# Activation buffers of 1280 instead of 1152 bytes, and operands of two stages placed in older buffers

## The chip, the cores and the metric

The kernel runs on one core of one Trainium2 chip. The metric is the device time of one execution in microseconds. The three runs before the change took 1665.74 to 1665.91 us, median 1665.88.

## The reference

One inference step (one layer) of a decoder with three parallel branches. Two groups of tokens share the weights: 256 of a prompt and 8 x 4 of samples, so all products have 288 columns.

```python
h = rms_norm(x, g_mix);  proj = h @ w_in
u_lin, u_gate, q_sb, k_sb, v_sb, q_mem, gate_logits = split(proj)
c = silu(layer_norm(causal_conv31(u_lin * sigmoid(u_gate))));  y_conv = c @ w_conv_out
y_sb  = stick_breaking_attention(q_sb, k_sb, v_sb, past pages) @ w_sb_out    # 8 heads
y_mem = softmax_attention(q_mem, memory) @ w_mem_out                         # 4 heads
g = sigmoid(gate_logits + b_gate)                                            # 3 x 2048
x = x + (g[0]*y_conv + g[1]*y_sb + g[2]*y_mem) @ w_o
x = x + square(relu(rms_norm(x, g_mlp) @ w_up)) @ w_down                     # 2048 -> 8192 -> 2048
```

All in float32. Besides the two groups' outputs the new keys and values, the last convolution inputs and the memory keys and values are returned.

## The kernel before

**Products.** Features lie on the 128 partitions, tokens along the free dimension (T = 288). Each float32 operand is split into a high part, rounded to fp32r, and the remainder, and a product is made of three: high x high, high weight x low activation, low weight x high activation. The weights stream from memory as 504 slabs of 128 x 1024 (8 blocks of 128 x 128), once each. `load_slab` brings one into a `wr` buffer; ScalarE rounds it (`cast_weights`, L295) into `wh`; VectorE subtracts (`sub_part`, L306) into `wl`. Four buffers of each rotate, so TensorE can be up to four slabs behind.

`main_tile` makes one 128 x 288 output tile in a PSUM bank (`pm`, four of them) from two slabs. `products` goes through a slab in 24 matmuls: for each of the 8 blocks the high weights with `a.h` and `a.l`, then the 8 low blocks with `a.h`. `chunk` (L467) issues them; the activation is the moving operand, 128 x 288, and the weight block the stationary one. Then an `evac` of VectorE, ScalarE or GpSimd empties the bank.

**Stages**, in the order of `main`: the memory's keys and values (`mem_products`, L518, in which the weights are the moving operand); the convolution's inputs; the heads of the memory attention and of the stick-breaking attention; the three gated branches (`branch_products` 2, 1, 0, in groups of four gates and four branch tiles); w_o (`out_tile`); and four times a block of 16 up tiles and 16 down tiles. The attentions over samples, the depthwise convolution (124 VectorE operations, L691 and L693) and the normalizations run beside them.

**Order.** A planner (`Order`) writes the order of the program: each piece of work is a generator that asks for an engine, a duration, flags that must be set, and buffers of a pool (`a=2`); the one that can start first is emitted. `give` returns buffers. Engines work in the order in which instructions were emitted.

**Buffers.** A pool holds equal buffers per partition. In address order: the constants, `wr` (4 of 4096 bytes), `a` (81 of 1152 bytes, one 288-column float32 tile each), `t` (11 of 1152, working tiles), `k4` (9 of 4096, pages of the caches), `s` (8 of 2048, attention rows), `wh` and `wl` (4 of 4096 each). `Acts` is a pair of `a` buffers for the high and low part. `hx` (the normalized input) holds 32 of them up to the last branch, `omem` and `osb` (the attentions' outputs) 8 and 16, `cact` (the convolution's) 8, `macc` (the gated sum, `branch`, L1229) 16; `merged` (L1242) takes 32. In the feed-forward `x1` holds 16, `h2` 32, and `u`, the squared output of `up_tile` (L1296 to L1304), 32, so that 80 of 81 are taken. `k4` and `s` serve the attentions and the convolution and are idle afterwards.

Of the kernel before, what the change touches and what calls it, by code (L numbers as in the profile page):

```python
# [7 lines left out]
F32 = mybir.dt.float32  # L8
F32R = mybir.dt.float32r
# [5 lines left out]
P = 128  # L15
D_MODEL = 2048
KT = D_MODEL // P
# [4 lines left out]
T = NP + NS  # L22
# [52 lines left out]
class Order:  # L75
# [15 lines left out]
    def add(self, gen, rank, at=None):  # L91
        job = Job(gen, rank, self.now.ready if at is None and self.now else at or 0.0)
        self.jobs.append(job)
        was, self.now = self.now, job
        self.step(job)
        self.now = was
# [10 lines left out]
    def give(self, pool, n=1):  # L107
        self.pools[pool] += [self.now.ready] * n
# [45 lines left out]
def dve(n, *flags, **take):  # L154
    return Ask("DVE", 0.18 + n / 920.0, flags, **take)


def act(n, *flags, **take):
    return Ask("ACT", 0.22 + n / 1200.0, flags, **take)


def pool(n, *flags, **take):
    return Ask("POOL", 0.3 + n / 420.0, flags, **take)


def pe(us, *flags, **take):
    return Ask("PE", us, flags, **take)


def sp(*flags, **take):  # L170
    return Ask("SP", 0.45, flags, **take)


VISIT = 4
MM = 0.1325
MM_MEM = 0.226
# [3 lines left out]
def tile_decoder_step(ctx: ExitStack, tc: tile.TileContext, xT, memT, wall, cvec, kmat, ptab,  # L180
# [1 line left out]
                      yT, oK, oV, oCp, oCs, oMK, oMV):  # L182
    nc = tc.nc
    PS = bass.MemoryType.PSUM
    bufs = {"wr": 4, "w": 4, "a": 81, "t": 11, "k4": 9, "s": 8, "pm": 4, "pa": 3, "pl": 1}

    def open_pool(name, n, space=None):
        if space is None:
            return ctx.enter_context(tc.tile_pool(name=name, bufs=n))
        return ctx.enter_context(tc.tile_pool(name=name, bufs=n, space=space))  # L190

    cpool = open_pool("const", 1)
    pools = {p: open_pool(p, n, PS if p in ("pm", "pa", "pl") else None) for p, n in bufs.items() if p != "w"}
    pools["wh"] = open_pool("wh", bufs["w"])
    pools["wl"] = open_pool("wl", bufs["w"])
    order = Order(bufs)
    give, add, done = order.give, order.add, order.set
# [3 lines left out]
    def tl(p, shape, dt=F32):  # L201
        cnt[0] += 1
        return pools[p].tile(shape, dt, tag=p, name=f"{p}_{cnt[0]}")
# [60 lines left out]
    class Slab:  # L264
        def __init__(self, parts):
            self.parts = parts
            self.landed = [Flag() for _ in range(parts)]
            self.split = [Flag() for _ in range(parts)]
# [12 lines left out]
    def due(s):  # L281
        return at_slab[1] + 2.9 * (s - at_slab[0])
# [32 lines left out]
    class Acts:  # L315


        def __init__(self, n=T):
            self.h, self.l = tl("a", [P, T], F32R)[:, :n], tl("a", [P, T], F32R)[:, :n]
            self.flag = Flag()  # L320

    hm, hx = [None] * KT, [None] * KT
# [305 lines left out]
    lin_done, gat_done, conv_done = ([Flag() for _ in range(CT)] for _ in range(3))  # L628
# [314 lines left out]
    def load_tiles(load, tiles, flags, which):  # L943
        for b in which:
            yield Ask("SP", 1.05, (pages_in,), k4=1)
            t, kb = load(b)
            tiles.append(t)
            flags[b].at = order.landed(kb) + 1.0
# [10 lines left out]
    def read_pages():  # L959

        for i in range(2 * NB):
            yield Ask("SP", 0.6, (pt_in,), 2.5)
            pages.append(nc.sync.value_load(pt[0:1, i:i + 1], min_val=0, max_val=kpool.shape[0] - 1))
        done(pages_in)
# [9 lines left out]
    def sample_values(load, aex, psum, x_T, new, first, cost):  # L974

        tiles, flags = [], [Flag() for _ in range(NB)]
        add(load_tiles(load, tiles, flags, range(0, VISIT)), 2)
        yield from x_T
        add(load_tiles(load, tiles, flags, range(VISIT, NB)), 2)
        if new is not None:  # L980
            yield from new
        for b in range(NB):
            if b % VISIT == 0:
                yield pe(VISIT * cost, *flags[b:b + VISIT], **({} if b else {"pl": 1}))
            if b == 0:
# [10 lines left out]
    def samples():  # L996
# [4 lines left out]
        for b in range(NB):  # L1001
            if b % VISIT == 0:
                yield pe(VISIT * 0.55, *flags[b:b + VISIT], *qm_made, **({} if b else {"pl": 1}))
            if b == 0:
# [30 lines left out]
    osb_in = [Flag() for _ in range(SH)]  # L1035
# [170 lines left out]
        yield from out_rows(out[0], [osb[h] for h in hs], [osb_in[h] for h in hs])  # L1206


    gates = {(br, j): Sigmoid() for br in range(3) for j in range(KT)}

    def gate(br, j):
# [9 lines left out]
    merged = [None] * KT  # L1221

    def branch(br, j):
        def evac(ps):
            sig = gates[br, j]
            if br == 2:
                yield dve(T, sig.flag, a=1)
                macc[j] = tl("a", [P, T])
                nc.vector.tensor_mul(macc[j], ps, sig.out)  # L1229
                give("pm")  # L1230
                give("t")
                return
            yield dve(T, sig.flag)
            nc.vector.tensor_mul(sig.out, ps, sig.out)  # L1234
            give("pm")
            yield dve(T)
            nc.vector.tensor_add(macc[j], macc[j], sig.out)
            give("t")
            if br == 0:
                yield act(T, a=2)  # L1240
                a = merged[j] = Acts()
                nc.scalar.copy(a.h, macc[j])  # L1242
                yield dve(T)
                nc.vector.tensor_sub(a.l, macc[j], a.h.bitcast(F32))
                give("a")
                done(merged_in[j])
        return evac
# [44 lines left out]
    def up_tile(u, f):  # L1292
        def evac(ps):
            yield dve(T, r2_done, t=1)
            r = tl("t", [P, T])
            nc.vector.scalar_tensor_tensor(r, ps, 0.0, r2, op0=ALU.max, op1=ALU.mult)  # L1296
            give("pm")
            yield pool(T)
            nc.gpsimd.tensor_mul(r, r, r)  # L1299
            yield act(T, a=2)  # L1300
            a = Acts()
            nc.scalar.copy(a.h, r)  # L1302
            yield dve(T)
            nc.vector.tensor_sub(a.l, r, a.h.bitcast(F32))  # L1304
            give("t")
            u[f].h, u[f].l = a.h, a.l
            done(u[f].flag)
        return evac
# [48 lines left out]
    def warm_up():  # L1357

        yield pe(4.2, pa=1)
        junk = bank("pa")  # L1360
        for i in range(7):
            nc.tensor.matmul(junk, warm[:, :P], warm[:, :512], start=True, stop=True)  # L1362
        give("pa")
        give("w")

    def main():
        yield from warm_up()
        yield from mem_products()
        yield from conv_products([evac_lin(0, "pa"), evac_gat(0, "pa"), evac_lin(1, "pm"), evac_gat(1, "pm")])
        for j in range(2, CT):  # L1370
            yield from main_tile(hx, evac_lin(j, "pm"))
            yield from main_tile(hx, evac_gat(j, "pm"))
        add(samples(), 3.0)
        for h in range(MH):
            yield from main_tile(hx, mem_head(h), 2 + 0.05 * h)
        for h in range(SH):
            yield from main_tile(hx, sb_key(h), 2.2 + 0.05 * h)
            yield from main_tile(hx, sb_query(h), 2.2 + 0.05 * h)
            yield from main_tile(hx, sb_head(h), 2.2 + 0.05 * h)
        yield from branch_products(2, [Late(omem, h, om_in[h]) for h in range(MH)])  # L1380
        give("a", 8)
        yield from branch_products(1, [Late(osb, h, osb_in[h]) for h in range(SH)])
        give("a", 16)
        yield from branch_products(0, [Late(cact, j, cact_flags[j]) for j in range(CT)])
        give("a", 40)
        mg = [Late(merged, j, merged_in[j]) for j in range(KT)]
        for j in range(KT):
            load, evac = out_tile(j)
            add(load(), 2)
            yield from main_tile(mg, evac)  # L1390
        give("a", 32)
        add(sum_norm(sq_sum, D_MODEL, r2, r2_done, sums_2), 0.4)
        hh = [Late(h2, j, h2_in[j]) for j in range(KT)]
        for c in range(D_FF // D_MODEL):
            u = [Later() for _ in range(KT)]
            for f in range(KT):
                yield from main_tile(hh, up_tile(u, f))
            for j in range(KT):
                yield from main_tile(u, down_tile(j, c == D_FF // D_MODEL - 1))
            give("a", 32)  # L1400

    def setup():
        yield dve(P, km_in)
# [4 lines left out]
    with tc.manual_schedule():  # L1408
        add(loads(), 1.0)
        add(cast_weights(), lambda: 0 if due(cast_at[0]) - order.free["ACT"] < 6.0 else 4.5)  # L1410
        add(mem_norm(), 0.6)
        add(sum_norm(x_sum, D_MODEL, rx, rx_done, sums_x), 0.6)
        add(main(), 20.0)
        add(conv_norm(), 8.0)
        add(setup(), 1.0)
        add(read_pages(), 4.0)
        order.run()
    assert slab_no[0] == wall.shape[0], slab_no

# [155 lines left out]
```

## Time and profile before

| | |
|---|---|
| median of three runs | 1665.88 us |
| profiled execution | 1665.56 us, its span 1663.8 us |
| TensorE busy | 1659.3 us (100%), 12,786 matmuls, granted clock 1.00 |
| VectorE, ScalarE, GpSimd busy | 992.3, 740.5, 138.9 us (60%, 45%, 8%) |
| memory traffic | 297.05 MB read, 6.32 MB written, 182 GB/s |
| weight rounding L295 | 520 on ScalarE, 1022 ns each |
| weight subtraction L306 | 520 on VectorE, 1195 ns each |

In the profile a line such as `L467 PE MATMUL pm<-a,wh 128*128 128x288 f32 x7744` names the line of the kernel, the engine, the operation, the output and the inputs by pool, the shape, and the number of instructions; behind it stand the busy time, the mean duration, and the idle time of the engine before these instructions with what ended it. PE is TensorE's matmul, PEld its weight load, DVE VectorE, ACT ScalarE, POOL GpSimd. The duration of a matmul is modelled and overlaps with the next one's. In the view by stages each row is a stretch of time: its length, TensorE's busy time with the number of its instructions in flight, its granted clock, the share and the rate of the DMA engines. In the timeline a row is a group of like instructions: start, length, name, count.

### The profile page before, as it was taken

The page shows a single profiled execution, that of the slowest core. Times are in us where ns is not written, and L with a number is a line of the kernel's source. Part 1 is how long each engine was busy: PE and PEld are TensorE (multiplying, and loading weights), DVE is VectorE, ACT ScalarE, POOL GpSimd, SP SyncE. Part 2 cuts the span into 40 slices and gives each one's busy share as a digit, 9 for nine tenths or more (in the row PEclk, how much of TensorE's full clock was granted, in tenths as well). Part 3 has the DMA queues.
Part 4 walks back from the last instruction along what each step waited for, and adds up shares of the span by engine and source line. Part 5 has one row for each costly group of instructions (what it writes and reads, how often), then busy time and mean ns, then how long its engine had stood idle before and what let it go on. Part 6 is the DMA issues. An engine that isn't in the chain of part 4 may idle for free.

```text
span 1663.8 us, 30938 instructions
## 1 busy us (share of the span) xinstructions
PE 1659.3 (100%) x12786; PEld 1639.9 (99%) x12786; DVE 992.3 (60%) x1470; ACT 740.5 (45%) x1071; POOL 138.9 (8%) x105
## 2 busy tenths in 40 slices
PE   9999999999999999999999999999999999999999
PEld 7999999999999999999999999999999999999999
DVE  8889888876777655565455544455444554445443
ACT  8746766644434534444443333333333333333332
POOL 0020000000000000001222200121001210022100
PEclk9999999999999999999999999999999999999999
DMA  9676464677755555556555555555555555555562
GB/s 335 210 178 248 140 215 155 200 244 278 285 186 166 167 171 166 165 156 203 186 172 165 166 168 163 166 167 171 161 168 164 166 166 166 165 165 165 177 189 98
DMA packets 107103, 305.39 MB, mean 184 GB/s; under 512 B 19922, under 2 KB 29522, under 8 KB 106962
## 3 DMA queue, kind: packets, MB, share of 16 engines
q1 hardware_dynamic: 106818, 303.39, 57.6%
q8 instruction: 100, 1.64, 0.4%
q14 instruction: 41, 0.34, 0.1%
q10 hardware_dynamic: 144, 0.02, 0.0%
HBM read 297.05 MB, written 6.32 MB: 182 GB/s over the span
## 4 chain that ended last, share of the span: by engine, by line
PE 100%; POOL 0%; DVE 0%; issue 0%; POOLq 0%
PE pm L467 93%; PE pm L518 3%; PE pa L467 1%; PE pl L991 1%; PE pl L1162 0%; PE pa L828 0%; PE pa L829 0%; PE pa L827 0%; PE pl L1007 0%; PE pa L1362 0%; PE pa L801 0%; PE pa L882 0%; PE pa L1118 0%; PE pa L1115 0%; PE pa L1117 0%; PE pa L1081 0%
## 5 line engine op out<-in xcount | busy, mean ns | idle before, releaser
L467 PE MATMUL pm<-a,wh 128*128 128x288 f32 x7744 | 1119.6, 295 | 0.0
L467 PEld LDWEIGHTS pm<-a,wh 128*128 128x128 f32 x7744 | 1057.5, 188 | 2.6 <-issue 2.4
L295 ACT CAST wh<-wr 128x1024 fp32r<-128x1024 f32 (+1 forms) x520 | 529.9, 1022 | 665.6 <-PE pm L467 623.2
L306 DVE TENSOR_TENSOR wl<-wr,wh 128x1024 fp32r<-128x1024 f32 (+1 forms) x520 | 619.8, 1195 | 203.6 <-ACT wh L295 202.3
L467 PE MATMUL pm<-a,wl 128*128 128x288 f32 x3872 | 598.4, 295 | 0.0
L467 PEld LDWEIGHTS pm<-a,wl 128*128 128x128 f32 x3872 | 541.7, 188 | 0.2 <-issue 0.2
L1299 POOL TENSOR_TENSOR t<-t 128x288 f32<-128x288 f32 x64 | 96.2, 1503 | 613.6 <-DVE t L1296 613.6
L1313 DVE TENSOR_TENSOR a<-a,pm 128x288 f32<-128x288 f32 x64 | 29.1, 454 | 127.3 <-PE pm L467 127.3
L1296 DVE SCALAR_TENSOR_TENSOR t<-pm,r 128x288 f32<-128x288 f32 x64 | 29.3, 457 | 97.4 <-PE pm L467 97.4
L1302 ACT CAST a<-t 128x288 fp32r<-128x288 f32 x64 | 27.6, 432 | 133.6 <-POOL t L1299 133.6
L1215 DVE TENSOR_TENSOR t<-pm,rx 128x288 f32<-128x288 f32 x48 | 22.0, 458 | 76.0 <-PE pm L467 75.9
L1304 DVE TENSOR_TENSOR a<-t,a 128x288 fp32r<-128x288 f32 x64 | 29.2, 458 | 63.4 <-ACT a L1302 63.4
L693 DVE SCALAR_TENSOR_TENSOR a<-a,cv,a 128x256 f32<-128x256 f32 x120 | 59.6, 496 | 1.5
L1285 POOL TENSOR_TENSOR t<-t,t 128x288 f32<-128x288 f32 x15 | 21.7, 1449 | 395.4 <-ACT t L1282 395.4
L518 PE MATMUL pm<-wh,a 128*128 128x512 f32 x128 | 35.9, 403 | 0.0
L518 PEld LDWEIGHTS pm<-wh,a 128*128 128x128 f32 x128 | 24.4, 193 | 6.3 <-ACT wh L295 0.9
L931 POOL MEMSET k<- 128x1024 f32 x6 | 5.7, 951 | 275.4 <-PE pl L1162 214.0
L1234 DVE TENSOR_TENSOR t<-pm,t 128x288 f32<-128x288 f32 x32 | 14.6, 458 | 21.1 <-PE pm L467 15.0
L1270 DVE TENSOR_TENSOR a<-pm,t 128x288 f32<-128x288 f32 x16 | 7.3, 458 | 29.9 <-PE pm L467 29.9
L219 ACT ACTIVATE t<-t,cv 128x288 f32<-128x288 f32 x48 | 21.8, 524 | 0.0
L518 PE MATMUL pm<-wl,a 128*128 128x512 f32 x64 | 20.3, 398 | 0.0
L680 POOL TENSOR_TENSOR k<-a,cv 128x992 f32<-128x992 f32 x4 | 10.9, 2741 | 74.0 <-DVE a L666 74.0
(198 smaller groups left out, 643.3 us busy)
## 6 DMA issues: line engine op xcount, KB each, us to landing
wr<-in_wall SPq DMA_DIRECT2D x488, 512.0 KB, 3.6
wr<-in_wall SPq DMA_DIRECT2D x32, 256.0 KB, 4.8
k<-in_kpool SPq DMA_DIRECT2D x32, 256.0 KB, 6.0
k<-in_vpool SPq DMA_DIRECT2D x32, 256.0 KB, 5.8
k<-in_mkc SPq DMA_DIRECT2D x8, 512.0 KB, 10.1
k<-in_mvc SPq DMA_DIRECT2D x8, 512.0 KB, 6.5
t<-in_xT SPq DMA_DIRECT2D x16, 144.0 KB, 3.7
out_yT<-a SPq DMA_DIRECT2D x16, 144.0 KB, 1.8
```

The lines of the kernel that those rows point to most:

```text
L219: nc.scalar.activation(out, src, func, **kw)
L295: nc.scalar.copy(sl.h[:, c], sl.raw[:, c])
L306: nc.vector.tensor_sub(sl.l[:, c], sl.raw[:, c], sl.h[:, c].bitcast(F32))
L467: nc.tensor.matmul(ps, w, a, start=(first and i == 0), stop=(last and i == len(todo) - 1))
L518: nc.tensor.matmul(ps[m], x[:, m * P:(m + 1) * P], y[:, w], start=(k == 0 and j < 2), stop=(k == KT - 1 and j in (4, 5)))
L693: nc.vector.scalar_tensor_tensor(c[:, :NP], up[:, k:k + NP], w, c[:, :NP], op0=ALU.mult, op1=ALU.add)
L1215: nc.vector.tensor_mul(g, ps, rx)
L1296: nc.vector.scalar_tensor_tensor(r, ps, 0.0, r2, op0=ALU.max, op1=ALU.mult)
L1299: nc.gpsimd.tensor_mul(r, r, r)
L1302: nc.scalar.copy(a.h, r)
L1304: nc.vector.tensor_sub(a.l, r, a.h.bitcast(F32))
L1313: nc.vector.tensor_add(x1[j], x1[j], ps)
```

## The change

An activation buffer of pool `a` gets 320 columns (1280 bytes) of which 288 are used, and there are 75 of them, not 81. A buffer of 128 bytes that nothing uses is put ahead of `t`. The operands `merged` and `u`, 32 tiles in turn, no longer come from `a`: once the convolution and the attentions over samples are done, `make_homes` takes all nine `k4` buffers, three operands in each at steps of 1280 bytes, and all eight `s` buffers, one in each, and makes sixteen fixed pairs (`homes`) of the first 32 parts. `branch` (for the last of the three branches) writes `merged[j]` to `homes[j]`; `up_tile` writes `u[f]` to `homes[f]`. The instructions that compute are the same ones.

```diff
+APART = 320
-    bufs = {"wr": 4, "w": 4, "a": 81, "t": 11, "k4": 9, "s": 8, "pm": 4, "pa": 3, "pl": 1}
+    bufs = {"wr": 4, "w": 4, "a": 75, "t": 11, "k4": 9, "s": 8, "pm": 4, "pa": 3, "pl": 1}
...
-    pools = {p: open_pool(p, n, PS if p in ("pm", "pa", "pl") else None) for p, n in bufs.items() if p != "w"}
+    pools = {}
+    for p, n in bufs.items():
+        if p == "t":
+            open_pool("gap", 1).tile([P, 32], F32, name="gap")
+        if p != "w":
+            pools[p] = open_pool(p, n, PS if p in ("pm", "pa", "pl") else None)
...
-            self.h, self.l = tl("a", [P, T], F32R)[:, :n], tl("a", [P, T], F32R)[:, :n]
+            self.h, self.l = tl("a", [P, APART], F32R)[:, :n], tl("a", [P, APART], F32R)[:, :n]
...
+    def make_homes():
+        yield sp(*conv_done, *osb_in, k4=bufs["k4"], s=bufs["s"])
+        parts = []
+        for _ in range(bufs["k4"]):
+            x = tl("k4", [P, 1024], F32R)
+            parts += [x[:, i * APART:i * APART + T] for i in range(3)]
+        for _ in range(bufs["s"]):
+            parts.append(tl("s", [P, 512], F32R)[:, :T])
+        for j in range(KT):
+            homes.append(Home(parts[2 * j], parts[2 * j + 1]))
+        done(homes_in)
...
-                yield act(T, a=2)
-                a = merged[j] = Acts()
+                yield act(T, homes_in)
+                a = merged[j] = homes[j]
...
-            yield act(T, a=2)
-            a = Acts()
+            yield act(T)
+            a = homes[f]
...
-        give("a", 32)
...
-            give("a", 32)
...
+        add(make_homes(), 1.0)
```

More of the change, by code (lines that the diff above doesn't have):

```diff
@@ L1206, in sb_sample, with __init__ @@
         yield from out_rows(out[0], [osb[h] for h in hs], [osb_in[h] for h in hs])
+    homes, homes_in = [], Flag()
+    class Home:
+        def __init__(self, h, l):
+            self.h, self.l = h, l
+    def make_homes():
[9 more added lines that the diff above has]
+        done(homes_in)
     gates = {(br, j): Sigmoid() for br in range(3) for j in range(KT)}
```

## The prediction

> **What bounds the kernel now.** I read the page first: the busy times, the granted clock, the chain that ended last, the costliest groups.
>
> ```profile
> span 1663.8 us, 30938 instructions
> PE 1659.3 (100%) x12786; PEld 1639.9 (99%) x12786; DVE 992.3 (60%) x1470; ACT 740.5 (45%) x1071; POOL 138.9 (8%) x105
> ...
> PEclk9999999999999999999999999999999999999999
> ...
> PE pm L467 93%; PE pm L518 3%; PE pa L467 1%; PE pl L991 1%; PE pl L1162 0%; PE pa L828 0%; PE pa L829 0%; PE pa L827 0%; PE pl L1007 0%; PE pa L1362 0%; PE pa L801 0%; PE pa L882 0%; PE pa L1118 0%; PE pa L1115 0%; PE pa L1117 0%; PE pa L1
> ...
> L467 PE MATMUL pm<-a,wh 128*128 128x288 f32 x7744 | 1119.6, 295 | 0.0
> L467 PEld LDWEIGHTS pm<-a,wh 128*128 128x128 f32 x7744 | 1057.5, 188 | 2.6 <-issue 2.4
> ```
>
> TensorE is never out of work: 100% busy, clock not throttled, no idle time before a matmul, and 94% of the chain is one line, L467, the 128x288 product. VectorE (60%) and ScalarE (45%) have room. So the time is the number of matmuls times their pace. The 295 ns of a row is a modelled, overlapped duration; the pace is the distance from one start to the next, which I took from the starts of all matmuls in the trace. The groups of L467 give the count:
>
> ```profile
> L467 PE MATMUL pm<-a,wh x7744: 288/295/406, 52.3 to 1659.2; 128*128 128x288 f32 x199
> L467 PE MATMUL pm<-a,wl x3872: 288/294/402, 52.8 to 1660.3; 128*128 128x288 f32 x194
> L467 PE MATMUL pa<-a,wh x64: 288/294/378, 50.7 to 74.9; 128*128 128x288 f32 x64
> L467 PE MATMUL pa<-a,wl x32: 288/295/298, 51.2 to 75.2; 128*128 128x288 f32 x32
> ```
>
> Together 11,712. For 11,591 of them the next matmul is L467 too and starts within 160 ns; these intervals sum to 1536.1 us, mean 132.52 ns. The other 121 stand at transposes, samples, and a few waits, nearly all in the first 480 us.
>
> Is the pace the same everywhere? The busy time by stage, with the stages cut at the first matmul of w_o and of each up and down block (768 products each; a window's count has some still in flight):
>
> ```profile
> 743.40:845.58 102.18, 102.18 (x770) 1.00 0.60 188
> ...
> 1049.36:1151.01 101.65, 101.65 (x770) 1.00 0.53 166
> 1151.01:1253.45 102.44, 102.44 (x770) 1.00 0.53 165
> 1253.45:1355.11 101.66, 101.66 (x771) 1.00 0.54 166
> 1355.11:1456.77 101.66, 101.66 (x771) 1.00 0.54 167
> 1456.77:1558.42 101.65, 101.65 (x770) 1.00 0.53 166
> 1558.42:1660.44 102.02, 102.02 (x770) 1.00 0.50 155
> ```
>
> The same 768 products with full buffers on every side, and 101.65 to 102.44 us (132.4 to 133.4 ns each). The up blocks (rows starting at 1049, 1253, 1457), which read the same h2 buffers, agree to 0.02 us; the down blocks (1151, 1355, 1558), each with other buffers for u, differ. So the pace depends on where the moving operand lies. The program's list of tile addresses says where: pool a starts at byte 33888 = 132 x 256 + 96 and steps by 1152 = 4.5 x 256, so its buffers lie at 96 or at 224 modulo 256; the weight buffers wh, wl all at 96. The interval after a matmul whose operand is at 96 has a mean of 131.66 ns (5,850 of the 11,591), at 224 133.41 ns (5,741). Finer splits (modulo 512 and more) add nothing: 131.62 and 131.70 at 96 and 352, 133.37 and 133.44 at 224 and 480.
>
> **The change, part by part.** *Does it do what it says?* By the sizes, yes: 75 x 1280 = 375 x 256 leaves the next pool at 96; the gap's 128 bytes and the eleven t buffers (12,672) make 50 x 256; k4, s, wh, wl move by 2816 = 11 x 256 and stay at 96; parts of a k4 buffer step by 1280. Every 288-column operand outside t is then at 96.
>
> *The pace of an all-96 stream.* The mean of 131.66 isn't it, since a matmul also shows what came before: a 96 after a 224 takes 130.8, a 96 between two 96 132.57 (1,604 cases). What is wanted is the pace deep in a run of equal ones. The longest run is eight, in the up blocks' second slab, 64 times; one of them is the middle of the x16 group here:
>
> ```profile
> 1083.24 1.22 PE L467 MATMUL pm<-a,wl 128*128 128x288 f32 x8
> 1084.29 2.29 PE L467 MATMUL pm<-a,wh 128*128 128x288 f32 x16
> 1086.42 1.22 PE L467 MATMUL pm<-a,wl 128*128 128x288 f32 x8
> 1087.48 0.29 PE L467 MATMUL pm<-a,wh 128*128 128x288 f32 x1
> ```
>
> (Start, length, group; 16 products from 1084.29 to 1086.42, then 8 to 1087.48.) Its eight intervals, as medians over the 64 repeats: 132, 136, 132, 131, 130, 135, 131, 131 ns. The eight low products behind it end in five at 96: 132, 130, 135, 131, 131. Sixteen runs of seven elsewhere: 131, 130, 135, 131, 131, 130, 135. After two or three products the same cycle of four stands each time, 131, 130, 135, 131, a sum of 527 ns: 131.75 each. Runs at 224 show 133, 132, 133, 136: 133.5. A few short 96 runs go otherwise (128, 133, 137, 127, 133: about 132.3), and all 548 intervals from the fourth place of a run on, its last left out, have a mean of 131.34, since they hold the cheap places of the cycle more often. I take 131.75, the whole cycle in the commonest and longest runs, and keep 131.34 and 132.57 as ends.
>
> Sum: 11,591 x 131.75 ns = 1527.1 us against 1536.1, **9.0 us less**; the ends give 13.7 less and 0.6 more.
>
> A rule to weigh here. The Trainium skill (TensorE: Matmul & The Clock Gate, section Back-to-back issue gap) gives a warm gap of N/2.4 + 2.5 ns, which for 288 columns would be an estimate of 122.5, with no term for the address; by it the change brings nothing. The trace stands 10 ns above that and does show the address, so I don't take it; what becomes of the time under it is a rival below. The same skill (SBUF — State Buffer, Specifications) counts 16-byte lines; 96 and 224 are both multiples of 16, so line counts would be equal as well, and the 1.75 ns between them is not explained by it.
>
> *The other products.* L518's moving operand is a weight slab, at 96 before and after; its 192 matmuls get a at 96 as the stationary side. I take 0 for them and for the small groups.
>
> *81 to 75 buffers.* The largest need outside the feed-forward is the end of the memory branch: hx 32, omem 8, osb 16, conv 4 and macc 16 make 76, one more while the last convolution tile holds its input.
>
> ```profile
> L693 DVE SCALAR_TENSOR_TENSOR a<-a,cv,a x120: 473/479/2422, 103.1 to 514.5; 128x256 f32<-128x256 f32 x120
> L1229 DVE TENSOR_TENSOR a<-pm,t x16: 447/457/459, 346.2 to 458.4; 128x288 f32<-128x288 f32 x16
> L1242 ACT CAST a<-a x16: 422/432/438, 645.6 to 744.6; 128x288 fp32r<-128x288 f32 x16
> ```
>
> L693 runs to 514.5, past L1229's 458.4, so both are live together: one or two of the last macc buffers now come from omem, and their multiply (L1229) waits until TensorE has done the branch's last tile, 12 products or 1.6 us each. Behind it in VectorE's queue stand the weight subtractions (L306) and the other evacuations; TensorE waits for those only if four split slabs (4 x 24 x 132.5 ns = 12.7 us) run out. I cost it at nothing; uncovered it is 2 x 1.6 = 3.2 us.
>
> *Old buffers for merged and u.* make_homes waits for the convolution (L693's last at 514.5) and the samples; the first write (L1242) is at 645.6, 131 us later, and no DMA or instruction is added on SP. In the feed-forward a write to homes[f] has to wait for the last down tile's read of it, which is ahead, on TensorE, of the up tile being evacuated. Three operands share a k4 buffer; if a write had to wait for a neighbour's, the last u of a block would come late: it is read 24 + 14 products (5.0 us) after the last up tile, and its chain is
>
> ```profile
> L1299 POOL TENSOR_TENSOR t<-t 128x288 f32<-128x288 f32 x64 | 96.2, 1503 | 613.6 <-DVE t L1296 613.6
> ...
> L1296 DVE SCALAR_TENSOR_TENSOR t<-pm,r 128x288 f32<-128x288 f32 x64 | 29.3, 457 | 97.4 <-PE pm L467 97.4
> L1302 ACT CAST a<-t 128x288 fp32r<-128x288 f32 x64 | 27.6, 432 | 133.6 <-POOL t L1299 133.6
> ...
> L1304 DVE TENSOR_TENSOR a<-t,a 128x288 fp32r<-128x288 f32 x64 | 29.2, 458 | 63.4 <-ACT a L1302 63.4
> ```
>
> 0.46 + 1.50 + 0.43 + 0.46 = 2.85 us, which leaves 2.1 us at each of five block starts. Nothing is charged.
>
> The profiled execution took 1665.56 us, 1.76 outside its span of 1663.8; the median of the runs is 1665.88. Forecast: span 1654.8, time 1665.88 - 9.0 = **1656.9**.
>
> **The rivals.** *The pace is conserved (no change).* If a 224 only moves time between neighbours, an alike stream costs what a mixed one does. For it: the 132.57 of a 96 between 96s, next to a mean of 132.52; and the 130.8 of a 96 just after a 224, as if time were paid back. Against it: the cycle of 131.75 returns in every long run, and 224 runs have one of 133.5. Price: 132.57 to 132.3, so +0.6 to -2.6 us: 1663.3 to 1666.5. The gap rule of the Trainium skill (TensorE: Matmul & The Clock Gate, section Back-to-back issue gap) points here too, with a pace that depends on the number of columns alone.
>
> *The stream locks into a slow cycle (slower).* The pace has a memory. In the second down block the same two operand patterns alternate, yet:
>
> ```profile
> 1157.35 2.32 PE L467 MATMUL pm<-a,wh 128*128 128x288 f32 x16
> 1159.52 1.22 PE L467 MATMUL pm<-a,wl 128*128 128x288 f32 x8
> 1160.58 2.28 PE L467 MATMUL pm<-a,wh 128*128 128x288 f32 x16
> 1162.70 1.23 PE L467 MATMUL pm<-a,wl 128*128 128x288 f32 x8
> 1163.76 0.42 PE L467 MATMUL pm<-a,wh 128*128 128x288 f32 x2
> ```
>
> The slab from 1157.35 to 1160.58 takes 3221 ns (intervals up to 153), while the block's very first slab, on the same operands, took 3170. An unbroken alike stream of 8,900 products from 480 us on could sit in such a state for good: 3221/24 = 134.2 ns, 11,591 x 1.69 = +19.6 us, 1685.5. It decides from a pace of 132.81 on (+3.3 us). Against it: none of the 548 intervals deep in runs of 96 is above 135.
>
> *More than forecast.* At 131.34 the gain is 13.7 us, 1652.2. It is in the range.
>
> **How the numbers follow.** About 0.2% (3.3 us) is what a measurement of this kernel can tell from no change. The alike stream's own faster cycle: 0.71, 1652 to 1661. Conserved pace: 0.20. Slow cycle, or a wait from the smaller pool and shared buffers that outweighs the gain: 0.09. That gives faster 0.71, same 0.20, slower 0.09. The range runs from the 131.34 end to the top of the conserved case, 1652 to 1666.
>
> **What would show it.** Right: the L467 count unchanged, no new idle time before it, and all nine stage windows of 768 products alike at 101.2 us, where they now differ by 0.8%; within a slab a cycle of four that sums to 527. The forecast is wrong if the stages are alike but at 101.8 (conserved) or 103 (slow cycle). The smaller pool would show as a wait of VectorE at L1229 near 455 us, followed by a wait of L467 for wl; shared buffers as gaps of TensorE at the block starts.

## The result, and the profile after

The change makes the kernel faster: 1655.36 us (median of six runs, 1654.85 to 1656.03) against 1665.87 (six runs, 1665.45 to 1665.91), a ratio of 0.9937 with a 95% interval of 0.9927 to 0.9947. That is 10.5 us or 0.6% less, where 9.0 us had been forecast.

The page of the changed kernel (line 467 is now 473; behind the engines' busy time stand share and instructions, then the granted clock, then the chain that ended last):

```profile
span 1654.0 us, 30953 instructions
PE 1648.8 (100%) x12786; PEld 1629.3 (99%) x12786; DVE 993.0 (60%) x1470; ACT 740.2 (45%) x1071; POOL 139.5 (8%) x105
...
PEclk9999999999999999999999999999999999999999
...
PE pm L473 93%; DMA wr<-in_wall 2%; PE pl L997 1%; PE pa L473 1%; PE pl L1168 0%; DMA s<-in_memT 0%; PE pa L834 0%; PE pa L835 0%; PE pa L833 0%; DVE wl L312 0%; PE pl L1013 0%; PE pa L807 0%; ACT a L364 0%; ACT wh L301 0%; PE pa L888 0%
```

The same 12,786 matmuls, TensorE as full as before, the other engines' busy time within 1 us of what it was: 9.8 us of span are gone without an idle time that could have gone. What became shorter is the distance between matmuls. The view by stages, cut as in the prediction (w_o, then up and down blocks in turn; length, TensorE busy with the products in flight, clock, DMA):

```profile
740.28:841.40 101.12, 101.12 (x770) 1.00 0.61 190
841.40:942.79 101.39, 101.39 (x773) 1.00 0.55 167
942.79:1043.91 101.12, 101.12 (x771) 1.00 0.55 168
1043.91:1145.03 101.12, 101.12 (x771) 1.00 0.54 166
1145.03:1246.15 101.12, 101.12 (x771) 1.00 0.55 168
...
1549.51:1650.63 101.12, 101.12 (x770) 1.00 0.50 157
```

Stages that differed by 0.8% before (101.65 to 102.44 us) are now equal to 0.01 us; the first up block is longer because two matmuls of the norm stand in it, as they did before. 101.12 us over 768 products are 131.67 ns. The 11,587 intervals of L473 counted as in the prediction sum to 1525.6 us (before, counted in this way: 11,589, 1535.8 us), 10.2 us less. With 0.2 us less in the first 50 us and 0.6 us more in two longer distances among the first products of L473 (at 52.7 and 53.1 us), that is the 9.8 us of the span.

Within a tile the alike slabs take the same time, here 3.16 us from one high group to the next (1081.83 to 1084.99); before, the slabs of the second down block, from its third on, alternated between 3.22 and 3.19 (the rows from 1157.35 to 1163.76 in the prediction):

```profile
1081.83 2.27 PE L473 MATMUL pm<-a,wh 128*128 128x288 f32 x16
1083.93 1.22 PE L473 MATMUL pm<-a,wl 128*128 128x288 f32 x8
1084.99 2.27 PE L473 MATMUL pm<-a,wh 128*128 128x288 f32 x16
```

### The profile page after: what moved, and what is told of

Same layout as the page of the kernel before. It is cut to its first block, busy times and chain, and to the rows that moved or that the text cites. A ratio compares the mean times of both kernels' runs of the same rounds, so it can differ in the third digit from the quotient of the medians.

```text
span 1654.0 us, 30953 instructions
## 1 busy us (share of the span) xinstructions
PE 1648.8 (100%) x12786; PEld 1629.3 (99%) x12786; DVE 993.0 (60%) x1470; ACT 740.2 (45%) x1071; POOL 139.5 (8%) x105
## 4 chain that ended last, share of the span: by engine, by line
PE 97%; DMA 2%; DVE 0%; ACT 0%; issue 0%; SPq 0%; DVEq 0%
PE pm L473 93%; DMA wr<-in_wall 2%; PE pl L997 1%; PE pa L473 1%; PE pl L1168 0%; DMA s<-in_memT 0%; PE pa L834 0%; PE pa L835 0%; PE pa L833 0%; DVE wl L312 0%; PE pl L1013 0%; PE pa L807 0%; ACT a L364 0%; ACT wh L301 0%; PE pa L888 0%
## 5 line engine op out<-in xcount | busy, mean ns | idle before, releaser
L301 ACT CAST wh<-wr 128x1024 fp32r<-128x1024 f32 (+1 forms) x520 | 529.6, 1021 | 656.6 <-PE pm L473 602.1
L473 PE MATMUL pm<-a,wh 128*128 128x288 f32 x5184 | 748.7, 294 | 0.1
L473 PEld LDWEIGHTS pm<-a,wh 128*128 128x128 f32 x5184 | 704.5, 188 | 2.9 <-issue 2.4
L473 PE MATMUL pm<-a,wl 128*128 128x288 f32 x2592 | 402.0, 294 | 0.0
L473 PEld LDWEIGHTS pm<-a,wl 128*128 128x128 f32 x2592 | 361.8, 188 | 0.2 <-issue 0.2
L473 PE MATMUL pm<-k,wh 128*128 128x288 f32 x2160 | 310.2, 294 | 0.0
L473 PEld LDWEIGHTS pm<-k,wh 128*128 128x128 f32 x2160 | 293.5, 188 | 0.0
L473 PE MATMUL pm<-k,wl 128*128 128x288 f32 x1120 | 173.2, 294 | 0.0
L473 PEld LDWEIGHTS pm<-k,wl 128*128 128x128 f32 x1120 | 156.6, 188 | 0.0
L473 PE MATMUL pm<-s,wh 128*128 128x288 f32 x400 | 65.9, 294 | 0.0
L473 PEld LDWEIGHTS pm<-s,wh 128*128 128x128 f32 x400 | 57.2, 188 | 0.0
L473 PE MATMUL pm<-s,wl 128*128 128x288 f32 x160 | 34.3, 296 | 0.0
```

The costliest lines, as they stand in the source:

```text
L301: nc.scalar.copy(sl.h[:, c], sl.raw[:, c])
L473: nc.tensor.matmul(ps, w, a, start=(first and i == 0), stop=(last and i == len(todo) - 1))
```

## The experiments

The gain being in the pace, the question is what sets the pace. Theory A is the prediction's: each residue of the moving operand's address modulo 256 has a pace of its own in a steady stream. Theory B: it counts only that all operands are alike. Theory C: what counts is the distance, modulo 256, between the moving operand and the weights that are loaded for the next product meanwhile. All kernels below are edits of the changed kernel, and each of the twelve was run beside the kernel before (1666.2 to 1666.4 us in these sets).

### Residue, likeness or distance

```diff
-            self.h, self.l = tl("a", [P, APART], F32R)[:, :n], tl("a", [P, APART], F32R)[:, :n]
+            self.h, self.l = tl("a", [P, APART], F32R)[:, 32:32 + n], tl("a", [P, APART], F32R)[:, 32:32 + n]
...
-            parts += [x[:, i * APART:i * APART + T] for i in range(3)]
+            parts += [x[:, i * APART:(i + 1) * APART] for i in range(3)]
...
-            parts.append(tl("s", [P, 512], F32R)[:, :T])
+            parts.append(tl("s", [P, 512], F32R)[:, :APART])
...
-            homes.append(Home(parts[2 * j], parts[2 * j + 1]))
+            homes.append(Home(parts[2 * j][:, 32:32 + T], parts[2 * j + 1][:, 32:32 + T]))
```

> The changed kernel with every operand of L473 shifted by 32 columns inside its 1280-byte slot: all moving operands at 224 modulo 256, weights still at 96. Theory A (each residue has its own steady pace; the runs at 224 in the trace of before showed 133.5 ns): mean interval 133.5 ns, nine stages of 768 products at 102.5 us, time near 1655.4 + 11.59 x 1.83 = 1676.6 us. Theory B (what counts is that all operands are alike, whichever residue): 131.67 ns, 101.1 us a stage, 1655.4 us. Theory C (what counts is the distance between moving operand and weights modulo 256, here 128): as A for this run.

Measured: 1675.58 us, ratio to the kernel before 1.0056 (1.0033 to 1.0079); mean interval 133.33 ns. Two of its stages (an up and a down block):

```profile
1056.32:1158.72 102.40, 102.40 (x771) 1.00 0.54 164
1158.72:1261.12 102.40, 102.40 (x771) 1.00 0.54 165
```

As alike as the changed kernel's stages, and 1.28 us longer each. Theory B falls: alike operands in the wrong place make the kernel slower than the mixture was.

The second shifts only the low parts (here and in the shifts below, `parts` are whole slots of 320 columns, as above).

```diff
-            self.h, self.l = tl("a", [P, APART], F32R)[:, :n], tl("a", [P, APART], F32R)[:, :n]
+            self.h, self.l = tl("a", [P, APART], F32R)[:, 0:0 + n], tl("a", [P, APART], F32R)[:, 32:32 + n]
...
+            homes.append(Home(parts[2 * j][:, 0:0 + T], parts[2 * j + 1][:, 32:32 + T]))
```

> The changed kernel with only the low parts (a.l) shifted by 32 columns: high parts at 96, low parts at 224, weights at 96, so that one product in three is at 224 in a fixed order. Theory A: a mean of the two residues' own paces, 131.67 x 2/3 + 133.5 x 1/3 = 132.3 ns, 1662.5 us. Theory B (mixing is what costs): 132.5 ns as in the kernel before, 1665.3 us. If the pace is conserved whatever the residue: 131.67 ns and 1655.4 us.

Measured: 1666.57 us, ratio 1.0002 (0.9991 to 1.0013); the up and down blocks behind the norm take 101.76 us, 132.50 ns, w_o ahead of it 101.97 us, 132.78 ns.

```profile
744.81:846.78 101.97, 101.97 (x770) 1.00 0.59 188
...
1050.59:1152.35 101.76, 101.76 (x771) 1.00 0.53 166
1152.35:1254.11 101.76, 101.76 (x771) 1.00 0.54 166
```

With a third of the products at 224 a mean of the two steady paces would be 132.22 ns (2/3 of 131.67, 1/3 of 133.33). The stream takes 0.28 ns more, or 0.56 in w_o, so paces don't simply average in a mixture; the kernel before had a mixture too, in no fixed order. Both paces come from the same order of operands (16 products with high and low parts in turn, then 8 with high parts): the stream has 132.78 ns in the 2,381 products from 539 us on and 132.50 in the 6,077 from 856 us on, and what lies between the two are two matmuls of the norm.

The third moves the weights and leaves the operands:

```diff
+    open_pool("wgap", 1).tile([P, 32], F32, name="wgap")
     pools["wh"] = open_pool("wh", bufs["w"])
```

> The changed kernel with 128 unused bytes ahead of the split weights: moving operands at 96, weights wh and wl at 224 modulo 256. Theory A (the moving operand's own residue): unchanged, 131.67 ns and 1655.4 us. Theory C (the distance between the two): the same pace as with all moving operands at 224, 133.5 ns and 1676.6 us by the runs in the trace of before. Theory B: 1655.4 us.

Measured: 1675.49 us, ratio 1.0056 (1.0033 to 1.0078), 133.33 ns.

```profile
1056.36:1158.76 102.40, 102.40 (x770) 1.00 0.53 164
1158.76:1261.16 102.40, 102.40 (x770) 1.00 0.54 165
```

The operands are where the changed kernel has them, at 96, and the time is that of the first experiment, to 0.1 us. Theory A falls, theory C stands. The counter-test moves both by 128 bytes (the two edits above together).

> The changed kernel with moving operands and weights both moved by 128 bytes, so that both lie at 224 modulo 256. Theory C (only the distance between the two counts): distance 0 again, 131.67 ns, 101.1 us a stage, 1655.4 us. If a residue of 224 itself costs for the one and the other reader: 133.3 ns or more, 1675 us or more.

Measured: 1655.16 us, ratio 0.9934 (0.9911 to 0.9956), 131.66 ns, against the changed kernel's 1655.36: no difference.

```profile
1043.29:1144.41 101.12, 101.12 (x771) 1.00 0.56 167
1144.41:1245.53 101.12, 101.12 (x771) 1.00 0.55 167
```

So 96 isn't a good residue and 224 a bad one. They are good or bad for weights that lie at 96. The slabs in `wr`, from which ScalarE and VectorE make the weights, lie at 96 in all these kernels, so that here they are 128 bytes from both operands and weights and in the changed kernel 0; with the same pace in both, the distance to them has no part in it.

### The parts of the change

Half of it: only merged and u in the old attention buffers; pool a with its 81 buffers of 1152 bytes, no gap.

```diff
-APART = 320
+APART = 288
...
-    bufs = {"wr": 4, "w": 4, "a": 75, "t": 11, "k4": 9, "s": 8, "pm": 4, "pa": 3, "pl": 1}
+    bufs = {"wr": 4, "w": 4, "a": 81, "t": 11, "k4": 9, "s": 8, "pm": 4, "pa": 3, "pl": 1}
...
-        if p == "t":
-            open_pool("gap", 1).tile([P, 32], F32, name="gap")
...
-            parts += [x[:, i * APART:i * APART + T] for i in range(3)]
+            parts += [x[:, i * 320:i * 320 + T] for i in range(3)]
```

> Half of the change: merged and u in the old attention buffers, all at 96, but pool a as before (81 buffers of 1152 bytes, at 96 or 224) and no gap. Theory A and B: the stages whose operands are merged or u (w_o and the four down blocks) go to 131.67 ns, 101.1 us each; the up blocks stay at 132.36 ns, 101.65 us; the stages before w_o keep 132.4. Gain over the kernel before (102.18 + 101.87 + 102.44 + 101.66 + 102.02) - 5 x 101.12 = 4.6 us, 1661.3 us. If the placement of merged and u itself cost waits, it would show here as more.

Measured: 1661.77 us, ratio 0.9973 (0.9962 to 0.9984). The rows are w_o, the first down, the second up and the second down block:

```profile
744.21:845.33 101.12, 101.12 (x771) 1.00 0.62 191
...
947.25:1048.37 101.12, 101.12 (x770) 1.00 0.54 168
1048.37:1150.03 101.66, 101.66 (x771) 1.00 0.53 166
1150.03:1251.15 101.12, 101.12 (x771) 1.00 0.55 168
```

Stage by stage as expected: those that read merged or u have the pace of the alike stream, the up blocks between them keep the old one, and a stage has its pace from its first tile on.

The other way round: all of the change but the alignment. With steps of 1152 bytes and no gap the weights lie at 96 and the operands at both residues.

```diff
-APART = 320
+APART = 288
...
-        if p == "t":
-            open_pool("gap", 1).tile([P, 32], F32, name="gap")
```

> Everything of the change but the alignment: 75 buffers, merged and u in the old attention buffers, but in steps of 1152 bytes, so that 6,824 products have their operand at 96 and 4,888 at 224; weights at 96. If alignment is the whole gain and the smaller pool and the shared buffers cost nothing: a mixed pace of 132.3 to 132.8 ns, 1663 to 1669 us, no change from the kernel before. If the new places bring something by themselves: well below 1663 us; if they cost waits: above 1669 us, with idle time of TensorE near 455 us or at the starts of blocks.

Measured: 1670.55 us, ratio 1.0026 (1.0015 to 1.0037), above the expected range. The loss is in the pace as well: the main line's intervals sum to 1540.2 us, 4.4 more than before the change, and the time is 4.3 us more.

```profile
745.28:847.46 102.18, 102.18 (x770) 1.00 0.62 188
1052.12:1154.31 102.19, 102.19 (x771) 1.00 0.53 164
1154.31:1256.49 102.18, 102.18 (x770) 1.00 0.54 166
```

TensorE's only waits before a matmul, 1.3 and 0.7 us, lie ahead of the main line's first product. So the smaller pool and the shared buffers cost nothing that can be seen, and this mixture is a worse one: w_o and the down blocks have 27% of their operands at 224 and take 133.05 ns; the up blocks of the kernel before had 52% and 132.36. The share doesn't tell the pace of a mixture. The order of the operands can, but not alone, as the half-shifted kernel's two paces show.

### Other distances

The gap ahead of the weights, or the shift of the operands, in smaller steps. First the weights 64 bytes further on, 64 back, 32 further on and 32 back (16, 48, 8 and 56 columns of gap):

```diff
+    open_pool("wgap", 1).tile([P, 16], F32, name="wgap")
```

> The changed kernel with 64 unused bytes ahead of the split weights: moving operands at 96, weights at 160 modulo 256 (64 further on). The runs before showed 131.67 ns at distance 0 and 133.33 ns at distance 128. If the pace rises evenly with the distance: 132.5 ns, 1665.2 us. If only the exact distance 0 is cheap: 133.3 ns, 1675 us. If some other distance is cheaper than 0 (two readers of the memory best kept apart): under 131.67 ns, down to 1655.4 - 11.59 x 0.83 = 1645.8 us for one step of 0.83 ns (the two paces known differ by two such steps).

> As e5 on the other side: weights at 32 modulo 256, 64 bytes behind the moving operands' 96. If only the size of the distance counts, the same pace as weights at 160; if its sign counts (which of the two readers is ahead), another one, 131.67 to 133.33 ns or below: 1645.8 to 1675 us.

> Weights at 128 modulo 256, 32 bytes further on than the moving operands. Even rise: 132.1 ns, 1660.3 us. Only distance 0 cheap: 133.3 ns, 1675 us. A better distance near 0: below 131.67 ns, 1645.8 us or more for one step.

> Weights at 64 modulo 256, 32 bytes behind the moving operands. Even rise: 132.1 ns, 1660.3 us. Only distance 0 cheap: 133.3 ns, 1675 us. A better distance near 0: below 131.67 ns, 1645.8 us or more for one step.

Then the operands 16 bytes ahead of the weights (a shift of 4 columns), and 16 behind (the same shift, and 8 columns of gap):

```diff
+            self.h, self.l = tl("a", [P, APART], F32R)[:, 4:4 + n], tl("a", [P, APART], F32R)[:, 4:4 + n]
...
+            homes.append(Home(parts[2 * j][:, 4:4 + T], parts[2 * j + 1][:, 4:4 + T]))
```

> Moving operands 16 bytes ahead of the weights modulo 256 (at 112, weights at 96). Seen so far: distance 0 131.67 ns, 64 ahead 131.67 to 132.22, 32 ahead 133.35, 128 133.33. If 133.33 ns is the common pace and a few distances save two steps of 0.83 ns: 133.33 ns and 1675 us, or 131.67 ns and 1655.4 us if 16 still counts as aligned. Below 131.67 ns, under 1655 us, only if distance 0 isn't the best one.

> Moving operands 16 bytes behind the weights modulo 256 (at 112, weights at 128). Same reckoning as for 16 ahead: 133.33 ns and 1675 us as the common pace, 131.67 ns and 1655.4 us if 16 bytes still count as aligned, less only if distance 0 isn't the best. If the two sides differ, the order of the two readers counts, not the size of the distance alone.

What they gave, with the runs above, by the distance of the operand from the weights:

| distance | operand, weights at | mean interval, ns | time, us | ratio to the kernel before |
|---|---|---|---|---|
| 0 | 96, 96 (the change) | 131.67 | 1655.36 | 0.9937 (0.9927 to 0.9947) |
| 0 | 224, 224 | 131.66 | 1655.16 | 0.9934 (0.9911 to 0.9956) |
| +16 | 112, 96 | 131.66 | 1657.24 | 0.9948 (0.9925 to 0.9970) |
| +32 | 96, 64 | 133.35 | 1676.21 | 1.0059 (1.0036 to 1.0082) |
| +64 | 96, 32 | 132.04 | 1661.06 | 0.9968 (0.9954 to 0.9981) |
| 128 | 224, 96 | 133.33 | 1675.58 | 1.0056 (1.0033 to 1.0079) |
| -64 | 96, 160 | 133.32 | 1675.23 | 1.0054 (1.0031 to 1.0077) |
| -32 | 96, 128 | 133.32 | 1676.00 | 1.0057 (1.0035 to 1.0080) |
| -16 | 112, 128 | 132.03 | 1659.83 | 0.9963 (0.9947 to 0.9978) |

No mean is below that of distance 0 by more than 0.01 ns, so none of these kernels beats the change. An even rise with the distance is refuted (+32 costs more than +64), and so is a single good distance: 133.33 ns is the steady pace at four of them, 131.67 that at 0 and nearly always at +16. The means at +64 and -16 are made of two paces each, and at +16 there is a second pace for three short stretches. At +64 (w_o, second up block):

```profile
742.38:843.50 101.12, 101.12 (x771) 1.00 0.62 190
...
1046.82:1148.36 101.54, 101.54 (x770) 1.00 0.54 166
```

At -16 (240 products near 490 us, second up block):

```profile
478.02:510.02 32.00, 32.00 (x243) 1.00 0.54 164
1046.18:1147.56 101.38, 101.38 (x771) 1.00 0.55 166
```

At +16 (48 products, second up block):

```profile
464.09:470.33 6.24, 6.24 (x51) 1.00 0.45 162
1045.34:1146.46 101.12, 101.12 (x770) 1.00 0.54 167
```

The same layout, two paces: at +64 the stream has 132.22 ns from 476 to 522 us, 131.67 from there to 852 us, and 132.22 again to the end; at -16 it has 133.33 ns from 475 to 521 us and 132.00 behind that; at +16 stretches of 34, 46 and 70 products, the last from 463 to 472 us, have 130.00 ns, and all else 131.67.

All these changes fall where other matmuls stand between the products (a single one at 475, two of the norm at 521, 522 and 852 us, longer groups of the attentions at both ends of the last stretch), and an unbroken stream keeps its pace. So at these three distances the pace depends on the distance and on how the stream began. At the others every stretch of 70 products or more came to one pace, within 0.1 ns. What sends a stream to the one or the other pace isn't shown. The 130.00 ns are the fastest that any stream here reached; over all 11,590 intervals they would be, as an estimate, 19 us less than 131.67, and nothing here shows how to stay there.

The sign counts too (+16 and -16, +64 and -64 differ). At +16 the products of the main line take as long as at 0. The profiled execution is 1.4 us longer, and 2.0 us more lie ahead of the first product (52.4 us against 50.5), in the loading and the memory products; TensorE's waits there for the rounded weights (L301) came to 2.2 us against 0.5. Why certain distances save 1.67 ns remains open; the runs show that the distance counts, not how the two reads meet.

## Why the prediction was right, and where its reasons weren't

**The bound** was right: the time followed the pace of L467 in every run, through a spread of 21 us between kernels that compute the same (19.8 us of it in the intervals of the main line, most of the rest ahead of its first product).

**The pace** was forecast as 131.75 ns and is 131.67; the 0.08 ns over 11,590 products are 1.0 of the 1.2 us by which the sum over the products was missed (10.2 for 9.0). The way to it was partly wrong. The members of the cycle of four (131, 130, 135, 131) that short runs at 96 showed aren't the steady ones: in the changed kernel twelve intervals return, 133, 126, 134, 134, 132, 127, 133, 135, 132, 127, 133, 134, with a sum of 1580 ns. They are three groups of four, alike within 1 ns, with sums of 527, 527 and 526, so the sum that the prediction named came true and its members didn't. Why short runs have the steady sum in another form isn't shown; that it could be carried over to an unbroken stream was in part luck. Runs at 224 had shown 133.5, and the steady stream has 133.33.

**The reason** was wrong in one step: "the pace depends on where the moving operand lies" leaves out the other reader. Weights all lay at 96 in the trace of before, so that its residues and its distances were the same thing, and nothing in it could have told them apart; the weights' shift did.

**The marginal means** (131.66 at 96, 133.41 at 224, each over a mixed stream) were rightly set aside as a proof, though they come out near the steady paces of both. That paces may be added up by share doesn't follow: in the half-shifted kernel that is 0.3 to 0.6 ns off.

**The conserved pace** falls: an alike stream at distance 0 is 0.86 ns below the mixture, one at 128 is 0.81 above. So does a pace that depends on the columns alone: with 288 columns throughout, the runs have steady paces of 130.00 to 133.33 ns. The formula that the prediction cites for it (the Trainium skill, TensorE: Matmul & The Clock Gate, Back-to-back issue gap) is given there for an isolated matmul, not for a stream with a weight load for each product, as here; its estimate of 122.5 ns is met by none of the runs.

**The slow cycle** did not come up in the changed kernel: its stream has 131.67 ns after every restart, and the slowest alike stream of all has 133.33, not 134.2. Its mechanism is real at other distances: at +16, +64 and -16 a stream settles into one of two paces and keeps it until other matmuls break it.

**The smaller pool** did make a wait where the prediction put it, and a short one. The rows are the macc multiplies (L1229 before, L1254 after) with VectorE's queue waiting ahead of them (minimum, median and maximum in ns). Before:

```profile
L1229 DVEq EVENT_SEMAPHORE  x12: 21/21/21, 345.8 to 456.8; - x12
```

After:

```profile
L1254 DVE TENSOR_TENSOR a<-pm,t x16: 448/455/460, 345.3 to 457.1; 128x288 f32<-128x288 f32 x16
L1254 DVEq EVENT_SEMAPHORE  x10: 21/21/276, 344.9 to 453.3; - x10
```

The longest is now 276 ns, not 1.6 us, and TensorE had no wait for it. The only new one before a matmul in the whole kernel is 0.5 us at the start, for the first weights; a weight load of L473 has a new one of 0.3 us at 53 us, for VectorE.

```profile
PE pa L1387 <- POOL eps L233: 1.3, 1, 1.3
PE pm L524 <- ACT wh L301: 0.5, 1, 0.5
```

**Old buffers for merged and u** cost nothing, as forecast: no stage has a gap at its start, and the half with nothing but them gained 4.4 us, where its stages' paces had given 4.6.

## What to carry to other kernels

Where TensorE is busy all the time, time can still lie in the distance between matmuls; compare stages that do the same work from different buffers, and take the starts, not the modelled durations. Look at the address of the moving operand together with that of the weights: put both at the same place modulo 256 bytes, and measure it, since alike operands at a wrong distance were 0.6% slower than no order at all. Look at a stream's pace after each of its interruptions too, since at some distances it settled at another one there. A mean over a mixed stream, sorted by one operand, points to the effect and doesn't price it: the sum comes from a stream that is alike throughout.

## What the runs showed of the hardware that was not expected

With 288 columns in fp32r and a weight load for each product, the pace of an alike stream took one of five values, 130.00 (for 150 products in all), 131.67, 132.00, 132.22 and 133.33 ns, the second and the last in a ratio of 79 to 80. The last had several patterns of single intervals: at a distance of -64 they alternate between 130 and 136 to 137, at -32 they repeat 133, 134, 133, and both means are 133.32. At three of the distances, +16, +64 and -16, which of two values it took changed where a few other matmuls broke the stream, and not within an unbroken one of up to 6,077 products. A mixed stream doesn't lie between them by its shares: the second down block before, with 44% of its operands at the distance of 128, took 133.39 ns, more than either; the third, with the same share in another order, took 132.37, and the up blocks with 52% took 132.36.
